# Token-major value projections: all 512 columns at once in four PSUM banks, instead of 256 columns per two heads

## The chip, the cores and the metric

The kernel runs on one core of a Trainium2 chip. The metric is the device time of one execution in microseconds. The median of three runs before the change is 1900.26 us (1900.05 to 1903.23).

## The reference, cut to what matters

Two layers of a hybrid block run over 256 latent tokens (`x`) and 256 context tokens (`y`), and a second block of feed-forward, recurrent and gating mixers follows them. Each layer projects the normalised tokens to queries, keys, values and gates of three attentions. The change touches the values of two of them, the retention (4 heads of 128 columns) and the neighbourhood attention (8 heads of 64 columns):

```python
rq, rk, rv, rg, nq, nk, nv, ng, gq, gk, gv, gg, mg = split_cols(hx @ w_in)
crq, crk, crv, crg, cnq, cnk, cnv, cng, cgq, cgk, cgv, cgg, cmg = split_cols(hy @ w_in)
o_lat, o_ctx = bidir_retention(heads(rq, 4), heads(rk, 4) * ksc, heads(rv, 4),
                               heads(crq, 4), heads(crk, 4) * ksc, heads(crv, 4), log_g, need_ctx)
na_x = neighbourhood_attention(heads(nq, 8), heads(nk, 8), heads(nv, 8), heads(cnk, 8), heads(cnv, 8), na_rpb, rows)
```

`rv` with `crv`, and `nv` with `cnv`, are each a product of 512 tokens by 1024 features with 1024 by 512 weights, once per layer.

## The kernel before

Matrices are kept to nearly fp32 precision as a high and a low part: a product is three matmuls (high by high, high by low, low by high), which `mm3` issues. Weights are loaded as `raw` tiles of 2048 columns (three buffers); `wsplit` makes the high part (`wh`) on ScalarE by a cast and the low part (`wl`) on VectorE by a subtraction, in pieces of 128 by 1024 (four buffers each). PSUM has eight tiles of 512 columns (`ps`), one bank each. Everything else lives in 60 tiles of 128 by 512 (`r`).

Most projections (`project`) put the weights in the array and stream tokens, so features come out on the partitions. Values are needed token-major, so `values` does it the other way round: a block of 128 tokens (`xh`, `xl`) stands in the array and the weights are streamed. It was called for two heads of the retention at once (tasks r0 and r2, 256 columns) and for two pairs of heads of the neighbourhood attention (tasks n0 and n2, 256 columns): four calls per layer, eight in all. In a call each of four token blocks takes 8 feature tiles, hence 4 x 8 x 3 = 96 matmuls of 256 columns; two token blocks share a bank. Each 256-column result is then split into high and low parts (`pair` for the retention, a strided `split` for the neighbourhood attention).

Tasks are generators: `t_ret` (r0 to r3), `t_na` (n0 to n3), `t_gkv` (gk) and `t_gqa` (g0 to g3, the grouped attention), `t_merge` (m0 to m2, gates and output projections of the three branches), `t_ada`. Layer 0 wants the order r, n, g, layer 1 the order r0 g0 r1 g1 and so on, then n. In layer 1 only the 256 latent tokens have queries. The recorder keeps every instruction with its dependencies, and a list scheduler with its own cost table then writes the order of each engine's queue; on the chip each queue is followed in that order. In layer 0 the first six projections of r0 and r1 (`lead`) accumulate in six banks ahead of everything else. Every instruction has the line of a helper, L335, so the trace is read by the tile names: `L0r` is layer 0's retention, `L1n` layer 1's neighbourhood attention, `L0m` its merges, `f`, `fa`, `fb`, `mix` the second block.

Of the kernel before, what the change touches and what calls it, by code (L numbers as in the profile page):

```python
# [13 lines left out]
P = 128  # L14
# [3 lines left out]
NK = D // P  # L18
# [21 lines left out]
def _turns(order, first, rate):  # L40
# [11 lines left out]
OFF = {  # L52
    "rq": 0, "rk": 512, "rv": 1024, "rg": 1536, "nq": 2048, "nk": 2560, "nv": 3072, "ng": 3584,
    "gq": 4096, "gk": 4608, "gv": 4736, "gg": 4864, "mg": 5376,
}
# [282 lines left out]
class _K:  # L338
# [22 lines left out]
    def ps(self):  # L361
        return self.tile("ps", 512)
# [213 lines left out]
    def values(self, l, c0, hx, stacked, out):  # L576


        (raw,) = self.wload([self.wk(self.a["w_in"][l], c0, 256)])
        ws = self.wsplit(raw[:, :4, :]) + self.wsplit(raw[:, 4:, :])  # L580
        for t2 in range(2):
            ps = self.ps()
            for t in range(2):
                tk = slice((2 * t2 + t) * P, (2 * t2 + t + 1) * P)
                for k in range(NK):
                    xh, xl = hx[k]
                    self.mm3(ps[:, 256 * t : 256 * t + 256], (xh[:, tk], xl[:, tk]), ws[k], k == 0, k == NK - 1)
            for t in range(2):
                src = ps[:, 256 * t : 256 * t + 256]
                if not stacked:  # L590
                    out.append(self.pair(src, 256))
                else:
                    v = self.r()
                    hl = v.rearrange("p (a x c) -> p a x c", a=2, x=4)
                    self.split(hl[:, :, 0::3, :], hl[:, :, 1:3, :], src.rearrange("p (a e c) -> p a e c", a=2, e=2))
                    out.append(v)
            yield 0

    def in_tiles(self, l, names):

# [65 lines left out]
    def ret_av(self, h, v, px, pc, nq):  # L666

        nc = self.nc
        col = P * (h % 2)
        vt = [(v[t][0][:, col : col + P], v[t][1][:, col : col + P]) for t in range(4)]  # L670
        o = self.ps()
        for kt in range(2):
            self.mm3(o[:, :nq], vt[2 + kt], (pc[kt][0][:, :nq], pc[kt][1][:, :nq]), kt == 0, False)
        for kt in range(2):
            c = slice(256 * kt, 256 * kt + 256)
            self.mm3(o[:, :T], vt[kt], (px[0][:, c], px[1][:, c]), False, kt == 1)
        oc, mu = self.f(), self.f()
        nc.scalar.copy(oc[:, :nq], o[:, :nq])
        nc.gpsimd.partition_all_reduce(mu[:, :nq], oc[:, :nq], channels=P, reduce_op=RED.add)
        self.stt(oc[:, :nq], mu[:, :nq], -1.0 / P, oc[:, :nq], ALU.mult, ALU.add)  # L680
        sq = self.f()
        self.act(sq[:, :nq], oc[:, :nq], AF.Square)
        nc.gpsimd.partition_all_reduce(mu[:, :nq], sq[:, :nq], channels=P, reduce_op=RED.add)
        return oc, mu
# [234 lines left out]
    def t_ret(self, l, h, hx, nq, S):  # L919
        yield from self.turn(S, "r", h)  # L920
        names = [(n, h) for n in ("rk", "rq", "rg")]
        led = self.led if l == 0 else {}
        raw = dict(zip([n for n in names if n not in led], self.in_tiles(l, [n for n in names if n not in led])))
        ps = lambda n, c: led[n, h] if (n, h) in led else self.project(raw[n, h], hx, c)

        def values():
            if h % 2 == 0:
                S["rv"] = v = []
                yield from self.values(l, OFF["rv"] + P * h, hx, False, v)

        if l == 0:
            yield from values()
            k = self.pair(ps("rk", T2), T2, KSC)
            yield 0
        q = self.pair(ps("rq", nq), nq)
        yield 0
        g = self.silu2(ps("rg", nq), nq)
        yield 0
        if l == 1:
            yield from values()  # L940
            k = self.pair(ps("rk", T2), T2, KSC)
            yield 0
        v = S["rv"]
        px, pc = self.ret_scores(l, h, q, k, nq)
        yield 6
        cen, vs = self.ret_av(h, v, px, pc, nq)
        S["done"] += 1
        yield 8
        S["o0"].append(self.ret_out(l, h, cen, vs, g, nq))

    def t_na(self, l, p, hx, nq, S):
        a = self.a
        yield from self.turn(S, "n", p)
        if p % 2 == 0:
            S["nv"] = v = []
            yield from self.values(l, OFF["nv"] + P * p, hx, True, v)
        v = S["nv"]
        wk, wq, wg = self.in_tiles(l, [("nk", p), ("nq", p), ("ng", p)])
        kp = self.project(wk, hx, T2)
        ks = [self.stack(kp, T2, r) for r in (0, 64)]  # L960
        yield 0
        qp = self.project(wq, hx, nq)
        qk = []
        los = self.zero_halves((0, 64), nq)
        for e, r in enumerate((0, 64)):
            qd = self.double(qp, nq, r, los[e][r : r + 64], 0.125)
            qk.append([(ks[e], qd), (ks[e], los[e])])
        yield 0
        g = self.silu2(self.project(wg, hx, nq), nq)
        yield 0  # L970
        pr = []
        for e in range(2):
            bias = self.tile("b", 384)
            self.nc.sync.dma_start(bias, a["na"][l, 2 * p + e])
            pr.append(self.scores(qk[e], nq, bias, 1.0, True))
            yield 3 if e == 0 else 14
        c0 = 256 * (p % 2)
        yield from self.attend(S, pr, v, (c0, c0 + P), g, nq, "o1", True)
# [659 lines left out]
```

## Time and profile before

| | before |
|---|---|
| median of three runs | 1900.26 us |
| the profiled execution | 1902.64 us, span 1900.9 us |
| TensorE matmul busy | 1858.4 us, 98% |
| VectorE busy | 1432.9 us, 75% |
| ScalarE busy | 1066.3 us, 56% |
| GpSimd busy | 209.7 us, 11% |
| mean granted TensorE clock | 0.994 of full speed |

The span runs from the first instruction to the last. Matmuls are pipelined and their ends are modelled, so a stream of matmuls is priced here by the distance from one start to the next and not by the mean duration of one. The two layers of the first block lie between about 64 us and 973 us; from there to the end the second block runs.

### The profile page before, as it was taken

How to read it: one execution, taken by the hardware profiler on the slowest of the kernel's cores; microseconds unless marked ns; L12 is line 12 of the kernel's file. 1: busy time of each engine (PE TensorE's matmuls, PEld its weight loads, DVE VectorE, ACT ScalarE, POOL GpSimd, SP SyncE). 2: the span in 40 equal slices, each digit the busy share in tenths (PEclk: the TensorE clock that was granted, in tenths of full speed). 3: DMA queues.
4: the chain of work that ended last, by engine and by line, in shares of the span. 5: the costliest groups of instructions: out<-in, count | busy, mean ns of one | idle time of the engine just before them, and what ended most of it. 6: DMA issues, size and time to landing. Idle time of an engine off the chain costs nothing.

```text
span 1900.9 us, 33415 instructions
## 1 busy us (share of the span) xinstructions
PE 1858.4 (98%) x13632; PEld 1739.5 (92%) x13632; DVE 1432.9 (75%) x2177; ACT 1066.3 (56%) x1704; POOL 209.7 (11%) x152
## 2 busy tenths in 40 slices
PE   6999999999999999999999999999999999999998
PEld 4888777777789889999999999999999999999998
DVE  7778978799857699999787668876656665777654
ACT  4656555656445597766565447754445444755443
POOL 0123323133300022222000000000000010000000
PEclk9999999999999999999999999999999999999999
DMA  9332443524343324434655566355555555545552
GB/s 321 119 97 93 128 148 101 155 88 123 102 153 100 89 78 116 124 106 146 209 178 188 190 194 200 111 201 187 179 183 180 188 181 193 190 157 176 181 188 98
DMA packets 336249, 291.95 MB, mean 154 GB/s; under 512 B 9184, under 2 KB 325728, under 8 KB 336096
## 3 DMA queue, kind: packets, MB, share of 16 engines
q1 hardware_dynamic: 336096, 289.82, 48.0%
q8 instruction: 107, 1.75, 0.4%
q14 instruction: 46, 0.38, 0.1%
HBM read 288.75 MB, written 1.05 MB: 152 GB/s over the span
## 4 chain that ended last, share of the span: by engine, by line
PE 87%; DVE 8%; ACT 2%; issue 1%; POOL 1%; DMA 0%; SPq 0%; DVEq 0%; POOLq 0%; ACTq 0%
PE fb_ps L335 13%; PE L0m_ps L335 7%; PE f_ps L335 7%; PE fa_ps L335 7%; PE L0n_ps L335 5%; PE L1m_ps L335 5%; PE L1r_ps L335 4%; PE L0r_ps L335 4%; PE fb1b_ps L335 3%; PE L1n_ps L335 3%; PE fa1b_ps L335 3%; PE fb0b_ps L335 3%; PE f0b_ps L335 3%; PE mix_ps L335 3%; PE L0out_ps L335 2%; PE L0in_ps L335 2%
## 5 line engine op out<-in xcount | busy, mean ns | idle before, releaser
L335 PE MATMUL fb_ps<-fb_r,fb_wh 128*128 128x256 f32 x1408 | 253.8, 283 | 0.0
L335 PEld LDWEIGHTS fb_ps<-fb_r,fb_wh 128*128 128x128 f32 x1408 | 219.6, 192 | 0.1
L335 PE MATMUL fb_ps<-fb_r,fb_wl 128*128 128x256 f32 x704 | 198.9, 283 | 0.0
L335 ACT CAST fb_wh<-fb_raw 128x1024 fp32r<-128x1024 f32 x88 | 92.2, 1047 | 123.0 <-PE fb_ps L335 89.3
L335 DVE TENSOR_TENSOR fb_wl<-fb_raw,fb_wh 128x1024 fp32r<-128x1024 f32 x88 | 107.7, 1224 | 65.1 <-ACT fb_wh L335 65.0
L335 PEld LDWEIGHTS fb_ps<-fb_r,fb_wl 128*128 128x128 f32 x704 | 135.0, 192 | 0.0
L335 PE MATMUL f_ps<-f_r,f_wh 128*128 128x256 f32 x704 | 127.2, 283 | 0.0
L335 PE MATMUL fa_ps<-fa_r,fa_wh 128*128 128x256 f32 x704 | 126.9, 283 | 0.0
L335 PE MATMUL L0m_ps<-L0in_r,L0m_wh 128*128 128x512 f32 x384 | 121.5, 395 | 0.0
L335 PEld LDWEIGHTS f_ps<-f_r,f_wh 128*128 128x128 f32 x704 | 109.8, 192 | 0.1
L335 PEld LDWEIGHTS fa_ps<-fa_r,fa_wh 128*128 128x128 f32 x704 | 109.8, 192 | 0.1
L335 PE MATMUL fa_ps<-fa_r,fa_wl 128*128 128x256 f32 x352 | 99.4, 283 | 0.0
L335 PE MATMUL f_ps<-f_r,f_wl 128*128 128x256 f32 x352 | 99.3, 283 | 0.0
L335 PEld LDWEIGHTS L0m_ps<-L0in_r,L0m_wh 128*128 128x128 f32 x384 | 71.9, 189 | 16.7 <-issue 1.6
L335 ACT CAST fa_wh<-fa_raw 128x1024 fp32r<-128x1024 f32 x44 | 46.1, 1047 | 63.5 <-PE fa_ps L335 39.7
L335 DVE TENSOR_TENSOR fa_wl<-fa_raw,fa_wh 128x1024 fp32r<-128x1024 f32 x44 | 53.8, 1224 | 35.4 <-ACT fa_wh L335 35.4
L335 POOL MEMSET mix_r<- 128x128 f32 (+1 forms) x36 | 7.7, 239 | 653.4 <-DVE fa_r L335 490.4
L335 DVE TENSOR_TENSOR L0g_r<-L0g_r,L0g_r 128x512 f32<-128x512 f32 (+3 forms) x116 | 72.4, 670 | 7.6 <-ACT L0g_r L335 5.4
L335 ACT CAST f_wh<-f_raw 128x1024 fp32r<-128x1024 f32 x44 | 46.1, 1048 | 56.4 <-PE f_ps L335 35.6
L335 PE MATMUL L0m_ps<-L0in_r,L0m_wl 128*128 128x512 f32 x192 | 75.0, 391 | 0.0
L335 ACT ACT_TABLE_LOAD x56 | 71.8, 1283 | 3.1 <-PE L0out_ps L335 1.4
L335 DVE TENSOR_TENSOR f_wl<-f_raw,f_wh 128x1024 fp32r<-128x1024 f32 x44 | 53.7, 1221 | 24.9 <-ACT f_wh L335 24.8
(506 smaller groups left out, 5729.7 us busy)
## 6 DMA issues: line engine op xcount, KB each, us to landing
fb_raw<-in_ffn_w_in_dram SPq DMA_DIRECT2D x44, 1024.0 KB, 5.2
f_raw<-in_ffn_w_in_dram SPq DMA_DIRECT2D x22, 1024.0 KB, 5.1
fa_raw<-in_ffn_w_in_dram SPq DMA_DIRECT2D x22, 1024.0 KB, 5.2
ada_raw<-in_ada_w_dram SPq DMA_DIRECT2D x32, 512.0 KB, 4.5
L0m_raw<-in_w_in_dram SPq DMA_DIRECT2D x24, 512.0 KB, 3.9
L1m_raw<-in_w_in_dram SPq DMA_DIRECT2D x24, 512.0 KB, 4.3
L0in_raw<-in_ada_w_dram SPq DMA_DIRECT2D x32, 256.0 KB, 6.0
f0b_raw<-in_ffn_w_out_dram SPq DMA_DIRECT2D x8, 1024.0 KB, 5.3
```

The costliest lines, as they stand in the source:

```text
L335: getattr(getattr(self.real, eng), method)(*a, **k)
```

## The change

`values` is called once per layer and attention, for all 512 columns (tasks r0 and n0), four calls in all instead of eight. It takes four banks at once, one for each token block. The weights come in two loads of four feature tiles by 512 columns; within one load, two feature tiles at a time go to all four banks, so the feature tiles are in the outer loop: 4 x 8 x 3 = 96 matmuls of 512 columns per call. The retention's results are split 512 columns at a time into two tiles, the neighbourhood attention's as before in 256-column pieces. r1 to r3 and n1 to n3 take their columns from what r0 and n0 left.

```diff
--- before.py
+++ after.py
@@ -576,25 +576,32 @@
     def values(self, l, c0, hx, stacked, out):
 
 
-        (raw,) = self.wload([self.wk(self.a["w_in"][l], c0, 256)])
-        ws = self.wsplit(raw[:, :4, :]) + self.wsplit(raw[:, 4:, :])
-        for t2 in range(2):
-            ps = self.ps()
-            for t in range(2):
-                tk = slice((2 * t2 + t) * P, (2 * t2 + t + 1) * P)
-                for k in range(NK):
-                    xh, xl = hx[k]
-                    self.mm3(ps[:, 256 * t : 256 * t + 256], (xh[:, tk], xl[:, tk]), ws[k], k == 0, k == NK - 1)
-            for t in range(2):
-                src = ps[:, 256 * t : 256 * t + 256]
-                if not stacked:
-                    out.append(self.pair(src, 256))
-                else:
+        w = self.a["w_in"][l]
+        pss = [self.ps() for _ in range(4)]
+        for k0 in range(0, NK, 4):
+            (raw,) = self.wload([self.wk(w, c0, 512, k0, 4)])
+            ws = self.wsplit(raw[:, :2, :]) + self.wsplit(raw[:, 2:, :])
+            for k2 in (0, 2):
+                for t, ps in enumerate(pss):
+                    tk = slice(t * P, (t + 1) * P)
+                    for k in (k0 + k2, k0 + k2 + 1):
+                        xh, xl = hx[k]
+                        self.mm3(ps, (xh[:, tk], xl[:, tk]), ws[k - k0], k == 0, k == NK - 1)
+            if k0 == 0:
+                yield 0
+        for ps in pss:
+            if not stacked:
+                out.append(self.pair(ps, 512))
+            else:
+                vs = []
+                for i in range(2):
                     v = self.r()
                     hl = v.rearrange("p (a x c) -> p a x c", a=2, x=4)
-                    self.split(hl[:, :, 0::3, :], hl[:, :, 1:3, :], src.rearrange("p (a e c) -> p a e c", a=2, e=2))
-                    out.append(v)
-            yield 0
+                    src = ps[:, 256 * i : 256 * i + 256].rearrange("p (a e c) -> p a e c", a=2, e=2)
+                    self.split(hl[:, :, 0::3, :], hl[:, :, 1:3, :], src)
+                    vs.append(v)
+                out.append(vs)
+        yield 0
 
     def in_tiles(self, l, names):
 
@@ -666,7 +673,7 @@
     def ret_av(self, h, v, px, pc, nq):
 
         nc = self.nc
-        col = P * (h % 2)
+        col = P * h
         vt = [(v[t][0][:, col : col + P], v[t][1][:, col : col + P]) for t in range(4)]
         o = self.ps()
         for kt in range(2):
@@ -924,9 +931,9 @@
         ps = lambda n, c: led[n, h] if (n, h) in led else self.project(raw[n, h], hx, c)
 
         def values():
-            if h % 2 == 0:
+            if h == 0:
                 S["rv"] = v = []
-                yield from self.values(l, OFF["rv"] + P * h, hx, False, v)
+                yield from self.values(l, OFF["rv"], hx, False, v)
 
         if l == 0:
             yield from values()
@@ -951,10 +958,10 @@
     def t_na(self, l, p, hx, nq, S):
         a = self.a
         yield from self.turn(S, "n", p)
-        if p % 2 == 0:
+        if p == 0:
             S["nv"] = v = []
-            yield from self.values(l, OFF["nv"] + P * p, hx, True, v)
-        v = S["nv"]
+            yield from self.values(l, OFF["nv"], hx, True, v)
+        v = [vs[p // 2] for vs in S["nv"]]
         wk, wq, wg = self.in_tiles(l, [("nk", p), ("nq", p), ("ng", p)])
         kp = self.project(wk, hx, T2)
         ks = [self.stack(kp, T2, r) for r in (0, 64)]
```

Three places show how the order of the queues moves. The first is TensorE's queue where layer 0's retention begins, right behind the last of the lead's matmuls (`L0in`); `L0r0_ps` are the banks of the values. Before:

```order
L335 MATMUL L0in_ps_35_127<-L0in_r_85_177,L0in_r_101_193 128x512
L335 MATMUL L0r0_ps_107_199<-L0r0_wh_103_195,L0in_r_25_117 128x256
L335 MATMUL L0r0_ps_107_199<-L0r0_wl_104_196,L0in_r_25_117 128x256
L335 MATMUL L0r0_ps_107_199<-L0r0_wh_103_195,L0in_r_26_118 128x256
L335 MATMUL L0r0_ps_107_199<-L0r0_wh_103_195,L0in_r_28_120 128x256
L335 MATMUL L0r0_ps_107_199<-L0r0_wl_104_196,L0in_r_28_120 128x256
L335 MATMUL L0r0_ps_107_199<-L0r0_wh_103_195,L0in_r_29_121 128x256
L335 MATMUL L0r0_ps_107_199<-L0r0_wh_103_195,L0in_r_44_136 128x256
L335 MATMUL L0r0_ps_107_199<-L0r0_wl_104_196,L0in_r_44_136 128x256
```

After:

```order
L335 MATMUL L0in_ps_35_127<-L0in_r_85_177,L0in_r_101_193 128x512
L335 MATMUL L0r0_ps_102_194<-L0r0_wh_107_199,L0in_r_25_117 128x512
L335 MATMUL L0r0_ps_102_194<-L0r0_wl_108_200,L0in_r_25_117 128x512
L335 MATMUL L0r0_ps_102_194<-L0r0_wh_107_199,L0in_r_26_118 128x512
L335 MATMUL L0r0_ps_102_194<-L0r0_wh_107_199,L0in_r_28_120 128x512
L335 MATMUL L0r0_ps_102_194<-L0r0_wl_108_200,L0in_r_28_120 128x512
L335 MATMUL L0r0_ps_102_194<-L0r0_wh_107_199,L0in_r_29_121 128x512
L335 MATMUL L0r0_ps_103_195<-L0r0_wh_107_199,L0in_r_25_117 128x512
L335 MATMUL L0r0_ps_103_195<-L0r0_wl_108_200,L0in_r_25_117 128x512
```

A bank got 48 matmuls of 256 columns in a row (two token blocks); now each of four banks gets six of 512 columns in turn, four rounds.

The second place is VectorE's queue in layer 0 where pair n1's probabilities are finished and n2 begins. `L0n2_wl` are the low parts of n2's weights, from `raw_404` the values' and from `raw_415` the keys' and queries'. Before:

```order
L335 TENSOR_TENSOR L0n1_r_370_462<-L0n1_r_362_454,L0n1_r_369_461 128x512
L335 TENSOR_TENSOR L0n1_r_366_458<-L0n1_r_363_455,L0n1_r_365_457 128x512
L335 TENSOR_TENSOR L0n0_r_374_466<-L0n0_ps_373_465,L0n0_r_374_466 64x512
L335 TENSOR_TENSOR L0n2_wl_406_498<-L0n2_raw_404_496,L0n2_wh_405_497 128x1024
L335 TENSOR_TENSOR L0n1_r_372_464<-L0n1_r_372_464,L0n1_r_363_455 128x256
L335 TENSOR_TENSOR L0n0_r_374_466<-L0n0_r_374_466,L0n0_r_300_392 128x512
L335 TENSOR_TENSOR L0n1_r_372_464<-L0n1_r_372_464,L0n1_r_363_455 128x256
L335 TENSOR_TENSOR L0n2_wl_408_500<-L0n2_raw_404_496,L0n2_wh_407_499 128x1024
L335 TENSOR_TENSOR L0n0_r_376_468<-L0n0_r_374_466,L0n0_r_375_467 128x512
L335 TENSOR_TENSOR L0n2_wl_419_511<-L0n2_raw_415_507,L0n2_wh_418_510 128x1024
```

After:

```order
L335 TENSOR_TENSOR L0n1_r_381_473<-L0n1_r_373_465,L0n1_r_380_472 128x512
L335 TENSOR_TENSOR L0n1_r_377_469<-L0n1_r_374_466,L0n1_r_376_468 128x512
L335 SCALAR_TENSOR_TENSOR L0n0_r_311_403<-L0n0_r_311_403,L0n0_r_295_387 128x512
L335 TENSOR_TENSOR L0n0_r_385_477<-L0n0_ps_366_458,L0n0_r_385_477 64x512
L335 TENSOR_TENSOR L0n0_r_385_477<-L0n0_ps_384_476,L0n0_r_385_477 64x512
L335 TENSOR_TENSOR L0n1_r_383_475<-L0n1_r_383_475,L0n1_r_374_466 128x256
L335 TENSOR_TENSOR L0n2_wl_419_511<-L0n2_raw_415_507,L0n2_wh_418_510 128x1024
L335 TENSOR_TENSOR L0n0_r_385_477<-L0n0_r_385_477,L0n0_r_311_403 128x512
L335 TENSOR_TENSOR L0n1_r_383_475<-L0n1_r_383_475,L0n1_r_374_466 128x256
L335 TENSOR_TENSOR L0n2_wl_424_516<-L0n2_raw_415_507,L0n2_wh_423_515 128x1024
```

The two splits of n2's value weights are gone from here (they stand ahead of n0 now), and the split of its key weights comes in their place.

The third place is TensorE's queue in layer 1 between the last scores of g0 (`L1g0_ps`) and the first scores of g1 (`L1g1_ps_1277`); `L1r2` is the third head's projections. Before:

```order
L335 MATMUL L1g0_ps_1269_1361<-L1g0_r_1248_1340,L1gk_r_1210_1302 128x256
L335 MATMUL L1g0_ps_1269_1361<-L1g0_r_1246_1338,L1gk_r_1210_1302 128x256
L335 MATMUL L1g0_ps_1269_1361<-L1g0_r_1248_1340,L1gk_r_1210_1302 128x256
L335 MATMUL L1g0_ps_1269_1361<-L1g0_r_1246_1338,L1gk_r_1210_1302 128x256
L335 MATMUL L1g1_ps_1277_1369<-L1g1_r_1265_1357,L1gk_r_1210_1302 128x256
L335 MATMUL L1g1_ps_1279_1371<-L1g1_r_1265_1357,L1gk_r_1210_1302 128x256
L335 MATMUL L1g1_ps_1287_1379<-L1g1_r_1266_1358,L1gk_r_1210_1302 128x256
L335 MATMUL L1g1_ps_1277_1369<-L1g1_r_1264_1356,L1gk_r_1210_1302 128x256
```

After:

```order
L335 MATMUL L1g0_ps_1280_1372<-L1g0_r_1257_1349,L1gk_r_1221_1313 128x256
L335 MATMUL L1g0_ps_1280_1372<-L1g0_r_1259_1351,L1gk_r_1221_1313 128x256
L335 MATMUL L1g0_ps_1280_1372<-L1g0_r_1257_1349,L1gk_r_1221_1313 128x256
L335 MATMUL L1r2_ps_1320_1412<-L0out_r_1064_1156,L1r2_wh_1321_1413 128x512
L335 MATMUL L1r2_ps_1320_1412<-L0out_r_1065_1157,L1r2_wh_1321_1413 128x512
L335 MATMUL L1r2_ps_1316_1408<-L0out_r_1064_1156,L1r2_wh_1317_1409 128x256
L335 MATMUL L1r2_ps_1316_1408<-L0out_r_1065_1157,L1r2_wh_1317_1409 128x256
L335 MATMUL L1r2_ps_1316_1408<-L0out_r_1064_1156,L1r2_wl_1318_1410 128x256
L335 MATMUL L1r2_ps_1316_1408<-L0out_r_1067_1159,L1r2_wh_1317_1409 128x256
L335 MATMUL L1r2_ps_1316_1408<-L0out_r_1068_1160,L1r2_wh_1317_1409 128x256
```

Before, the scores of g1 follow those of g0 directly. Now fifteen matmuls of r2's projections stand between them, two of 512 columns and thirteen of 256, and behind g1's scores r2's values, 96 matmuls of 256 columns, are gone.

## Rows read from the trace of the kernel before

**Rows 1.** The page: busy time of each engine, and the granted clock in 40 slices.

```profile
PE 1858.4 (98%) x13632; PEld 1739.5 (92%) x13632; DVE 1432.9 (75%) x2177; ACT 1066.3 (56%) x1704; POOL 209.7 (11%) x152
...
PEclk9999999999999999999999999999999999999999
```

**Rows 2.** The page: chain that ended last, shares of the span by engine.

```profile
PE 87%; DVE 8%; ACT 2%; issue 1%; POOL 1%; DMA 0%; SPq 0%; DVEq 0%; POOLq 0%; ACTq 0%
```

**Rows 3.** Windows of the first block: stretch, length, busy us, granted clock, DMA.

```profile
core 0: us, PE busy (x) PEld busy (x) DVE busy (x) ACT busy (x) POOL busy (x), PEclk, DMA share, GB/s
64.50:184.00 119.50, 119.50 (x701) 105.12 (x700) 89.68 (x119) 62.94 (x95) 34.38 (x15) 1.00 0.30 91
184.00:222.00 38.00, 35.16 (x205) 26.57 (x204) 37.84 (x51) 23.66 (x40) 18.23 (x8) 1.00 0.37 110
222.00:395.00 173.00, 171.53 (x892) 136.84 (x891) 141.82 (x195) 97.02 (x152) 43.45 (x23) 1.00 0.42 127
...
683.00:697.00 14.00, 10.78 (x61) 10.27 (x61) 12.68 (x32) 12.21 (x24) 2.43 (x2) 0.76 0.27 75
697.00:816.00 119.00, 118.30 (x876) 112.51 (x876) 112.09 (x181) 89.17 (x159) 25.84 (x23) 1.00 0.40 115
```

**Rows 4.** Groups by shape, TensorE: the value matmuls of layer 0's retention.

```profile
L335 PE MATMUL L0r_ps<-L0r_wh,L0in_r 128*128 128x256 f32 x128 | 23.7, 283 | 0.0
...
L335 PE MATMUL L0r_ps<-L0r_wl,L0in_r 128*128 128x256 f32 x64 | 18.1, 283 | 0.0
```

**Rows 5.** The chain in order of time: start us, us, what; unbroken streams of one shape.

```profile
474.89 16.32 PE L0m_ps L335 x72
...
894.17 56.16 PE L1m_ps L335 x468
```

**Rows 6.** The chain again, from 60 to 260 us: the lead's end and n2's start.

```profile
59.80 4.76 PE L0in_ps L335 x21
...
64.56 15.72 PE L0r_ps L335 x120
...
220.38 27.37 PE L0n_ps L335 x158
```

**Rows 7.** Timeline of VectorE and ScalarE: start us, us, instruction, idle before.

```profile
63.72 0.68 DVE L335 TENSOR_TENSOR L0r_r<-L0in_ps,L0r_r 128x512 fp32r<-128x512 f32 x1
...
152.37 0.42 DVE L335 TENSOR_TENSOR L0n_r<-L0n_ps,L0n_r 128x256 fp32r<-128x256 f32 x1
...
164.22 1.21 DVE L335 TENSOR_TENSOR L0n_wl<-L0n_raw,L0n_wh 128x1024 fp32r<-128x1024 f32 x1
...
150.84 0.37 ACT L335 CAST L0n_r<-L0n_ps 128x256 fp32r<-128x256 f32 x1
...
156.67 1.28 ACT L335 ACT_TABLE_LOAD   x1
```

**Rows 8.** Timeline of TensorE: its longer waits, in brackets the idle time and releaser.

```profile
206.44 0.62 PE L335 MATMUL L0n_ps<-L0n_r,L0n_r 128*128 128x256 f32 x3 [1.01 <-DVE L0n_r L335]
...
217.98 0.39 PE L335 MATMUL L0n_ps<-L0n_wl,L0in_r 128*128 128x256 f32 x1 [0.37 <-DVE L0n_wl L335]
...
421.21 0.67 PE L335 MATMUL L0g_ps<-L0g_r,cstt 128*128 128x256 f32 x2 [3.55 <-DVE L0g_r L335]
...
508.05 0.80 PE L335 MATMUL L0m_ps<-L0g_r,L0m_wh 128*128 128x512 f32 x1 [3.82 <-ACT L0g_r L335]
...
687.95 0.50 PE L335 MATMUL L1g_ps<-L1g_r,L1gk_r 128*128 128x256 f32 x2 [1.86 <-ACT L1g_r L335]
```

**Rows 9.** Window of n2 of layer 0, columns as in group 3.

```profile
222.00:250.00 28.00, 28.00 (x169) 23.91 (x168) 22.60 (x32) 11.81 (x20) 2.47 (x3) 1.00 0.42 131
```

## The prediction

> **What bounds the kernel now.** I read the page first: TensorE is busy 98% of the span, VectorE 75%, ScalarE 56%, and the granted clock is full in every slice [rows 1]. Busy time of pipelined matmuls overstates, so the second view is the chain of work that ended last: 87% of it is TensorE, 8% VectorE [rows 2]. The reader is to see that a microsecond of matmul work taken out is mostly a microsecond off the span, except where TensorE waits. The third view, windows of the first block, says where that is [rows 3]: from 64.5 to 184 us TensorE has no gap; from 184 to 222 it lacks 2.84 us while VectorE is busy 37.84 of 38.00; from 683 to 697 it lacks 3.22 us and the granted clock falls to 0.76. The timeline names the larger single waits, and I come to them with the moves.
>
> **What is removed.** Layer 0's retention issues 128 + 64 = 192 value matmuls of 256 columns [rows 4]; there are four such groups (two layers, two attentions), so 768 matmuls of 256 columns become 384 of 512. Prices come from unbroken streams on the chain [rows 5]: 72 matmuls of 512 columns took 16.32 us, 0.2267 us each; 468 of 256 took 56.16 us, 0.1200 us each. Two of 256 cost 0.2400, so each pair saves 0.0133 us. Hence 768 x 0.1200 = 92.16 us, 384 x 0.2267 = 87.05 us, saving 5.1 us, 1.28 us per group. The new loop goes to another bank every six matmuls; the lead already does that with 512 columns, and its last 21 took 4.76 us, again 0.2267 each [rows 6], so I add nothing for it. The bounds of this term are 0 (if a value matmul of 512 columns took twice 0.1200) and 5.1; I take 5.1, because both prices are of these very shapes.
>
> The page "TensorE: Matmul & The Clock Gate" of the Trainium skill, section "Back-to-back issue gap", puts the isolated distance at columns / 2.4 GHz plus about 2.5 ns. By it a pair would save only 2.5 ns and the change 1.0 us, an estimate from that page. The streams here do not agree: they stand 13.3 ns above columns / 2.4 GHz at both widths, so the measured rows decide.
>
> **What costs nothing.** *Banks:* the lead holds six of eight. Values start at 64.56 [rows 6], the third bank is wanted 12 x 0.2267 = 2.7 us later. Four of the lead's banks have been read out by 63.72 + 0.68 = 64.4 us [rows 7], so four are there. Without that cover the price is the delay of the readout, up to about 2 us. *Readout:* the retention's results take four VectorE subtractions of 512 columns (0.68) for eight of 256 (0.42) per layer [rows 7], 2.7 us for 3.4; nobody waits for values at once, the scores come first. *ScalarE:* the queue holds 54 table loads for 56, at 1.28 us [rows 7]; ScalarE is idle 44% of the time. *Loads:* the same bytes, in two loads of the same size, the second pulled ahead to r0 or n0; the transfers' share is 0.27 to 0.42 in the windows of the first block [rows 3]. *Second block:* from the first feed-forward on, the queues are in the same order on every engine.
>
> **What moves.** Each group takes 96 x 0.1200 = 11.5 us of TensorE work, with 2 x 1.21 + 4 x 0.42 = 4.1 us of VectorE work [rows 7], from r2 or n2 to r0 or n0. Everything between the two starts 96 x 0.2267 - 96 x 0.1200 - 1.28 = 9.0 us later in the second attention of a layer and 10.2 in the first; behind r2 or n2 TensorE is level again, less the saving. Two places matter, because VectorE is nearly full there.
>
> *n2 of layer 0.* TensorE waits 1.01 us for n1's probabilities and 0.37 for n2's value weights [rows 8]. n1 is the same work for both engines, only later, so those waits stay. Behind it stood the value matmuls, the first 96 of the 158 in the stream of 27.37 us [rows 6], in which VectorE could catch up. VectorE has 28.00 - 22.60 = 5.4 us free from 222 to 250 [rows 9], and 4.1 us of work leaves. TensorE could stand 11.5 - 5.4 - 4.1 = 2.0 us; the bounds are 0 and 11.5 - 4.1 = 7.4 (VectorE without any free time). The queue puts n2's key weights straight where the value weights were, which speaks for the low end: I take +1.
>
> *r2 of layer 1.* From 697 to 816 VectorE is busy 112.09 of 119.00 [rows 3], so 6.9 us are free, over a longer stretch; bounds again 0 and 7.4. Key and gate projections of r3, g2 and n0 can be pulled forward, I take +1. Just ahead of it, g1's scores wait 1.86 us at 687.95 [rows 8]; now fifteen of r2's projections (13 x 0.1200 + 2 x 0.2267 = 2.0 us) stand in that gap. The whole hole is 14.0 us for 61 matmuls [rows 3], at most 14.0 - 61 x 0.1200 = 6.7 us with the fallen clock; bounds 0 and 6.7. I take -2, the fill itself.
>
> The two long waits of layer 0 (3.55 us at 421, 3.82 at 508 [rows 8]) belong to the grouped attention, whose distances in the queue stay as they were: 0.
>
> **Sum.** -5.1 + 1 + 1 - 2 = -5.1 us. The profiled execution took 1902.64 us (span 1900.9), 2.4 above the median; it should become 1897.5, the median 1900.26 - 5.1 = 1895.2 us.
>
> **Rivals.** 0.2% of the time, 3.8 us, is about what a measurement of this kernel can tell from no change: faster is below 1896.5, slower above 1904.1.
>
> 1. *The saving arrives, the waits cancel* (the forecast): 1892 to 1896.4. For it: 98% and 87% TensorE.
> 2. *A wait takes part of it back:* the 2.0 us at n2, 2.0 at r2 and nothing gained at g1, 1900.26 - 5.1 + 4.0 = 1899.2. For it: VectorE 37.84 of 38.00; against it: the work ahead of those waits shrinks by 4.1 us too.
> 3. *The hole in layer 1 closes:* up to 6.7 us more, 1900.26 - 5.1 - 6.7 = 1888.5. For it: the fill; against it: the ScalarE chain that g1 waits for is no shorter.
> 4. *The change does not do what it says:* a value matmul of 512 columns costs as much as two of 256, saving 0, 1900.3. Against it: the same shapes in the streams. By the page cited above the time would be 1899.3, an estimate; the streams speak against it too.
> 5. *Slower:* at r2 of layer 1 VectorE is the limit and there is no filler. From 683 to 697 waits of 3.22 us made a hole of up to 6.7, since the granted clock fell: a wait there costs about twice its length. The forecast turns to slower once r2's waits pass (5.1 + 3.8) / 2 = 4.5 us; at 5 us the time is 1900.26 - 5.1 + 10 = 1905.2. For it: VectorE's 112.09 of 119.00; against it: the projections that can be pulled forward.
>
> **Chances.** Forecast 0.45, the second 0.30, the third 0.13, the fourth 0.03, slower 0.09 (its point is far, but VectorE is near it). Faster is 0.45 + 0.13 = 0.58, the same 0.30 + 0.03 = 0.33, slower 0.09. The range 1890 to 1901.5 leaves out the slower case, about a third of the third case and the upper end of the second, under 0.2 in all.
>
> **What would show it.** 13632 - 384 = 13248 matmuls, value groups of 96 with 512 columns and a distance of 0.2267 us between starts; a longer distance makes the first term wrong. In layer 0 no new wait at about 67 us; at the start of n2's projections a wait of at most 2 us. In layer 1 g1's scores wait less than 1.86 us, and no clock below full between r2 and n0; a fallen clock there is the slower case. The stretch from the end of the first block on stays as long as it was; if it changes, the prediction is wrong for a reason that I have not seen.

## The result, and the profile after

The changed kernel took 1913.72 us (median of four runs, 1912.11 to 1914.71) against 1901.72 us: a ratio of 1.0062, interval 1.0045 to 1.008. It is slower by 12 us where 5 us faster were forecast. The profiled execution took 1914.71 us, its span is 1912.9 us.

The page after, in the lines that answer to [rows 1, 2]:

```profile
PE 1860.5 (97%) x13248; PEld 1724.8 (90%) x13248; DVE 1436.6 (75%) x2169; ACT 1063.4 (56%) x1694; POOL 195.9 (10%) x152
...
PE   6999999999999999989999999999999999999998
...
PE 86%; DVE 7%; ACT 3%; issue 1%; DMA 1%; POOL 0%; SPq 0%; DVEq 0%; ACTq 0%; POOLq 0%
```

The 384 matmuls are gone, yet busy shares and chain look as before. One digit of the page hints at the loss: in the 18th of its 40 slices, from 813 to 861 us, TensorE is busy 8 tenths (before: 9). Where the 12 us went is told by two marks in the timeline: the last output projection of layer 0 (`L0m`) and that of layer 1 (`L1m`) on TensorE. From the first value matmul to the first mark, and from there to the second, each in the profiled execution:

| | layer 0, us | layer 1, us |
|---|---|---|
| before | 502.7 | 382.9 |
| after | 501.7 | 395.5 |

Layer 0 gained 1.0 us, layer 1 lost 12.5. Behind it nothing changed.

The waits of TensorE after, its longest groups: engine and tile, what it waited for, us in total, times, longest.

```profile
PE L1n_ps L335 <- DVE L1n_r L335: 6.5, 1, 6.5
PE L1g_ps L335 <- ACT L1g_r L335: 3.9, 2, 2.6
PE ada_ps L335 <- DMA ada_raw<-in_ada_w_dram: 3.8, 1, 3.8
PE L0n_ps L335 <- ACT L0n_r L335: 3.6, 1, 3.6
```

The timeline of TensorE after, values first, then the long waits:

```profile
64.87 0.39 PE L335 MATMUL L0r_ps<-L0r_wh,L0in_r 128*128 128x512 f32 x1
...
69.86 0.39 PE L335 MATMUL L0r_ps<-L0r_wl,L0in_r 128*128 128x512 f32 x1
...
697.31 0.51 PE L335 MATMUL L1g_ps<-L1g_r,L1gk_r 128*128 128x256 f32 x2
...
700.91 0.75 PE L335 MATMUL L1g_ps<-L1g_r,L1gk_r 128*128 128x256 f32 x4 [0.58 <-DVE L1gk_r L335]
...
704.46 0.55 PE L335 MATMUL L1g_ps<-L1g_r,L1gk_r 128*128 128x256 f32 x1 [2.57 <-ACT L1g_r L335]
...
757.19 0.50 PE L335 MATMUL L1g_ps<-L1g_r,L1gk_r 128*128 128x256 f32 x2 [1.36 <-ACT L1g_r L335]
...
849.36 0.77 PE L335 MATMUL L1n_ps<-L0out_r,L1n_wh 128*128 128x256 f32 x2 [6.45 <-DVE L1n_r L335]
```

Between the first two rows lie 22 matmuls with three changes of bank: 4.99 / 22 = 0.2268 us each, as in the streams of before [rows 5]. So the width does what it should, and there is no wait at its start. The last row is the new thing: in layer 1, a projection of pair n2 waits 6.45 us for VectorE.

The rows between are told apart by count, since each pair of the grouped attention has 16 score matmuls and g0's end at 694.5 us. The 16 of g1 begin at 697.31, and only the last four of them wait, 0.58 us: the projections put in front of them did fill the wait of 1.86 us [rows 8]. The matmul at 704.46 is the first product of g0's probabilities with the values. It waits 2.57 us for ScalarE, which still works on g0's softmax; before, r2's projections and r2's values were TensorE's work during that time.

Windows of layer 1 after (columns as in [rows 3]):

```profile
697.00:710.00 13.00, 9.79 (x47) 8.05 (x46) 12.58 (x27) 11.92 (x23) 2.86 (x4) 0.74 0.14 40
750.00:770.00 20.00, 16.79 (x108) 15.60 (x106) 18.00 (x33) 17.49 (x33) 6.36 (x6) 0.83 0.19 57
...
780.00:800.00 20.00, 20.00 (x90) 16.58 (x89) 17.15 (x29) 10.94 (x21) 1.06 (x1) 1.00 0.37 106
800.00:810.00 10.00, 10.00 (x75) 9.52 (x74) 4.27 (x6) 4.67 (x8) 0.31 (x1) 1.00 0.08 19
810.00:849.00 39.00, 32.78 (x229) 30.45 (x227) 38.60 (x64) 27.37 (x50) 8.74 (x7) 0.97 0.44 126
...
845.00:850.00 5.00, 0.64 (x3) 0.67 (x4) 4.91 (x9) 3.61 (x8) 0.00 (x0) 0.66 0.26 82
850.00:855.00 5.00, 5.00 (x31) 5.00 (x31) 4.01 (x10) 1.20 (x3) 1.79 (x1) 0.66 0.07 23
```

The first five stretches before:

```profile
697.00:710.00 13.00, 13.00 (x105) 12.69 (x105) 11.63 (x20) 12.83 (x25) 4.01 (x4) 1.00 0.43 122
750.00:770.00 20.00, 19.47 (x153) 18.50 (x152) 19.78 (x36) 19.46 (x35) 5.50 (x6) 1.00 0.46 133
...
780.00:800.00 20.00, 20.00 (x143) 18.78 (x142) 19.39 (x33) 14.14 (x26) 1.68 (x1) 1.00 0.39 118
800.00:810.00 10.00, 10.00 (x67) 9.16 (x66) 9.91 (x17) 6.65 (x11) 2.40 (x4) 1.00 0.51 149
810.00:849.00 39.00, 38.03 (x293) 36.65 (x292) 38.37 (x67) 23.75 (x47) 9.68 (x6) 1.00 0.32 94
```

Read these in pairs. From 697 to 710 TensorE was busy throughout before; now it lacks 3.21 us and the granted clock falls to 0.74. From 800 to 810, behind n0's values, while n0's other projections run, VectorE now idles (busy 4.27 of 10 us, in the same time before 9.91); then it is full for 39 us, and TensorE, which was busy 38.03 us in that time before, is busy 32.78.

The chain that led to the wait after, start, us, what:

```profile
810.88 0.70 DVE L1n_r L335
...
838.17 2.04 DVE L1n_r L335 x3
840.21 1.14 DVE L1m_wl L335
...
842.02 1.26 DVE L1n_r L335 x3
...
847.48 1.01 DVE L1n_r L335 x2
...
848.52 0.70 DVE L1n_r L335
...
849.36 6.82 PE L1n_ps L335 x40
```

From 810.88 to the end of the wait it runs on VectorE almost alone. What TensorE waits for is a bank: in the compiled program n2's gate projection takes the bank that held n2's keys. The instruction at 848.52 is the last that reads them, a split that stands behind n1's softmax in VectorE's queue. The 40 matmuls behind the wait took 6.82 us instead of 40 x 0.12 = 4.80, since the granted clock had fallen (0.66 from 845 to 855): the hole costs 6.45 + 2.0 = 8.5 us.

### The profile page after: what moved, and what is told of

Its sections match the earlier page's. It is cut to its first block, busy times and chain, and to the rows that moved or that the text cites. A ratio compares the mean times of both kernels' runs of the same rounds, so it can differ in the third digit from the quotient of the medians.

```text
span 1912.9 us, 32631 instructions
## 1 busy us (share of the span) xinstructions
PE 1860.5 (97%) x13248; PEld 1724.8 (90%) x13248; DVE 1436.6 (75%) x2169; ACT 1063.4 (56%) x1694; POOL 195.9 (10%) x152
## 4 chain that ended last, share of the span: by engine, by line
PE 86%; DVE 7%; ACT 3%; issue 1%; DMA 1%; POOL 0%; SPq 0%; DVEq 0%; ACTq 0%; POOLq 0%
PE fb_ps L335 13%; PE L0m_ps L335 8%; PE f_ps L335 7%; PE fa_ps L335 7%; PE L0n_ps L335 6%; PE L1m_ps L335 5%; PE L0r_ps L335 4%; PE L1r_ps L335 3%; PE fb1b_ps L335 3%; PE fa1b_ps L335 3%; PE fb0b_ps L335 3%; PE f0b_ps L335 3%; PE L1n_ps L335 3%; PE mix_ps L335 3%; PE L0out_ps L335 2%; PE L0in_ps L335 2%
## 5 line engine op out<-in xcount | busy, mean ns | idle before, releaser
L335 DVE TENSOR_TENSOR L0g_r<-L0g_r,L0g_r 128x256 f32<-128x256 f32 (+3 forms) x116 | 74.9, 687 | 8.2 <-ACT L0g_r L335 5.6
L335 PE MATMUL L1m_ps<-L0out_r,L1m_wh 128*128 128x256 f32 x384 | 72.8, 286 | 0.0
```

Source lines behind the costliest of these rows:

```text
L335: getattr(getattr(self.real, eng), method)(*a, **k)
```

## The experiments

Three theories stood at the start. *Cover*: the value matmuls at r2 and n2 were what TensorE did while VectorE and ScalarE worked on the scores; without them it waits. *The loop*: four banks, bank changes and wide readouts cost wherever they stand. *The plan*: the scheduler's order shifts as a whole, and no part has a price. Ratios are to the kernel before, run beside each.

**e1, e2, e3: one part of the change each.** `values2` is the old function; e1 has the sets below, e2 `{"r": (1,), "n": ()}`, e3 `{"r": (), "n": (1,)}`.

```diff
+WIDE = {"r": (0,), "n": (0,)}
...
-            if h == 0:
+            if h == 0 and l in WIDE["r"]:
                 S["rv"] = v = []
                 yield from self.values(l, OFF["rv"], hx, False, v)
+            elif h % 2 == 0 and l not in WIDE["r"]:
+                S["rv"] = v = []
+                yield from self.values2(l, OFF["rv"] + P * h, hx, False, v)
```

> Layer 0 has the new values (512 columns at r0 and n0), layer 1 the old ones (256 columns at r0, r2, n0, n2). Theory (the loss is made in layer 1, where work that filled TensorE beside a busy VectorE was taken away from r2 and n2): layer 0 ended 0.5 us earlier after the change, so this kernel takes about 1901.2 us against 1901.7, no difference. Rival (the new loop itself costs, by four banks held at once, a bank change every six matmuls, or the results read 512 columns at a time): two of the four groups carry half of the 12 us, 1907.7 us.

Measured: 1899.96 us, ratio 0.9987 (0.9977 to 0.9996).

> Only the retention of layer 1 has the new values. In the trace after the change TensorE lost 10.9 us against the price of its matmuls from 640 us to the first value matmuls of n0, before 3.6 us. Theory: this group alone carries 7.3 - 1.3 = 6.0 us, 1907.7 us, and the holes lie between g0 and g3. Rival (the new loop itself): a quarter of 12 us, 1904.7 us. Second rival (the whole plan shifts, no part has a cost of its own): any other number, and the parts do not add up to 12.

Measured: 1907.35 us, ratio 1.0026 (1.0016 to 1.0036). Its timeline has the holes of the changed kernel at the same places:

```profile
705.84 0.55 PE L336 MATMUL L1g_ps<-L1g_r,L1gk_r 128*128 128x256 f32 x1 [2.57 <-ACT L1g_r L336]
...
758.57 0.50 PE L336 MATMUL L1g_ps<-L1g_r,L1gk_r 128*128 128x256 f32 x2 [1.36 <-ACT L1g_r L336]
```

> Only the neighbourhood attention of layer 1 has the new values. In the trace after the change TensorE lost 9.4 us against the price of its matmuls from n0's values to 912 us, before 1.7 us in the same stretch of the program. Theory: this group alone carries 7.7 - 1.3 = 6.4 us, 1908.1 us, with a wait of 5 to 7 us for VectorE behind n1. Rival (the new loop itself): a quarter of 12 us, 1904.7 us. Second rival (the whole plan shifts): the three parts do not add up to 12.

Measured: 1909.06 us, ratio 1.0036 (1.0023 to 1.0049), with a wait of 6.44 us behind n1. In the profiled executions layer 1 is 6.7 us longer in e2 and 5.5 in e3, together 12.2 of the 12.5; layer 0 is 3.3 us shorter in e1. Such lengths, from one execution each, are uncertain by 2 to 3 us: e1 and the changed kernel have the same order of matmuls in layer 0 and differ by 2.3 us there, and e2's profiled execution took 3.2 us more than its median. By the ratios the parts are -2.5, +4.9 and +6.9 us, together 9.3, where the whole is 11.8; the difference lies within the intervals. So the parts add up as far as can be told, and nothing is left that only the plan as a whole would explain. Equal shares per group are out: the change in layer 0 alone is a gain.

**e4: the move without the width.**

```diff
+                if h == 0:
+                    S["rvs"] = [[], []]
+                    for i in range(2):
+                        yield from self.values(l, OFF["rv"] + 256 * i, hx, False, S["rvs"][i])
+                S["rv"] = S["rvs"][h // 2]
```

(the same for n, with p)

> The old loop with 256 columns, two banks and token blocks outside, but both calls stand at r0 and at n0, as in the changed kernel: the move alone, 768 matmuls of 256 columns. Theory (the move costs 17 us, the width gives 5.1 back): 1913.7 + 5.1 = 1918.8 us, between 1917 and 1921. Rival (the new loop itself costs): about 1901.7 us, as before.

Measured: 1919.84 us, ratio 1.0087 (1.0072 to 1.0102). The old loop at the new places costs the most, so the place is the cause and the loop is not. The width gives back the difference to the changed kernel: in ratios 0.0025 x 1902 = 4.8 us, where 5.1 were computed (the two intervals together allow 0.4 to 9).

**e7: two banks at a time.**

```diff
-        pss = [self.ps() for _ in range(4)]
+        ws, pss = [], []
         for k0 in range(0, NK, 4):
             (raw,) = self.wload([self.wk(w, c0, 512, k0, 4)])
-            ws = self.wsplit(raw[:, :2, :]) + self.wsplit(raw[:, 2:, :])
+            ws += self.wsplit(raw[:, :2, :]) + self.wsplit(raw[:, 2:, :])
+        for t2 in range(2):
+            two = [self.ps() for _ in range(2)]
...
```

> The changed kernel, but its values take two banks at a time: all eight feature tiles of 512 columns are split first, then the token blocks 0 and 1 are multiplied, then 2 and 3; 384 matmuls of 512 columns as in the changed kernel, at the same places. Theory (the move to r0 and n0 costs): no difference from 1913.7 us beyond 2 us. Rival (four banks held at once take the banks from the projections): 5 us or more below it, 1908 us or less.

Measured: 1913.12 us (1909.88 to 1914.91), ratio 1.0051 (1.0036 to 1.0066). No difference, and the same wait in its list:

```profile
PE L1n_ps L335 <- DVE L1n_r L335: 6.5, 1, 6.5
```

**e9, e10: other work for TensorE in the old places.** `fill` multiplies token tiles by each other into two banks that nobody reads.

```diff
+    def fill(self, hx):
+        for t2 in range(2):
+            ps = self.ps()
...
+                    self.mm3(ps[:, 256 * t : 256 * t + 256], (xh[:, tk], xl[:, tk]), (xh[:, :T], xl[:, :T]), k == 0, k == NK - 1)
...
+        if l == 1 and p == 2:
+            self.fill(hx)
+            yield 0
```

> The kernel of e3 (new values in the neighbourhood attention of layer 1 alone, 1909.1 us) with 96 extra matmuls of 256 columns ahead of n2's projections, where the old values stood: token blocks by token blocks, into two banks that nobody reads, no weights, no VectorE or ScalarE work; 96 x 0.12 = 11.5 us of added TensorE work. Theory (TensorE has no work to cover the softmax of n1, a chain through VectorE, GpSimd and ScalarE): the added work lies in the hole of 6.4 us and the 1.9 us of fallen clock behind it, so it costs only 11.5 - 8.3 = 3.2 us: 1912.3 us, and the wait behind n1 is under 1 us. Rival (the chain is tied to what TensorE does, and moves with it): 1909.1 + 11.5 = 1920.6 us.

Measured: 1912.01 us, ratio 1.0044 (1.0029 to 1.0059) against e3's 1.0036: 11.5 us of added matmuls cost about 1.5 us by the ratios (4.3 by the length of layer 1). Nothing waits at n2 any more (a merge ahead of it waits 1.07 us), and the chain runs through n2 on TensorE alone:

```profile
830.37 26.58 PE L1n_ps L336 x200
856.95 2.88 PE L1m_ps L336 x24
```

This is the plainest evidence for cover: work that touches no other engine fits into the hole.

> The kernel of e2 (new values in the retention of layer 1 alone, 1907.4 us) with the same 96 extra matmuls behind r2's gate projection, where the old values stood; 11.5 us of added TensorE work. In e2 TensorE lost about 7.3 us more than before between g0 and g3. Theory (cover, as at n2): most of the loss goes, 1907.4 + 11.5 - 6 = 1913 us, between 1911.5 and 1915. Rival (in the retention the loss has another cause than missing cover, as the order of the queues between g1 and r2): 1907.4 + 11.5 = 1919 us.

Measured: 1914.99 us, ratio 1.0062 (1.0047 to 1.0077) against e2's 1.0026: 0.0036 x 1903 = 6.9 us for 11.5, so 4.6 us of the loss is cover, at the upper edge of what was expected. The wait of g0's product, 2.57 us in e2, is gone. Part of the loss stays: g1's scores, ahead of the fill, wait again, and so does a merge behind r2:

```profile
697.72 1.22 PE L336 MATMUL L1g_ps<-L1g_r,L1gk_r 128*128 128x256 f32 x8 [1.37 <-DVE L1g_r L336]
...
772.23 0.50 PE L336 MATMUL L1m_ps<-L1r_r,L1m_wh 128*128 128x256 f32 x2 [2.19 <-ACT L1r_r L336]
```

**e5: useful work as cover.** To e3 is added:

```diff
+for _p, _m in enumerate((0, 4, 8, 12)):
+    TURN[1]["n"][_p] = (TURN[1]["n"][_p][0], _m)
```

> The kernel of e3 (new values in the neighbourhood attention of layer 1 alone; +6.5 us), with one more edit: in layer 1 the pairs n0 to n3 begin after 0, 4, 8 and 12 steps of the merges, not after -4, 0, 4 and 8. Four merge steps, 4 x 48 x 0.12 = 23.0 us of matmuls with about 2.4 us of VectorE work each, come ahead of n1 instead of behind n3. Theory (the wait of 6.4 us behind n1 is VectorE's lag, because the moved value matmuls no longer give TensorE work while VectorE catches up): any other filler serves too; VectorE gains 23.0 - 9.6 = 13.4 us on TensorE, the wait and the fallen clock behind it (6.4 + 1.9 us) go, and the time comes to about 1901, between 1899 and 1903. Rival (the wait is made by the four banks held at once, or by the readout in 512 columns): the new loop is the same, 1909 us.

Measured: 1901.34 us, ratio 0.9991 (0.9982 to 1.0001). 0.0045 x 1902 = 8.6 us better than e3, with the same loop at the same place.

**e6, e13: what the wait hangs on.** The order of every queue is that of the changed kernel; instructions are cut as they are issued, so most scores keep their maximum (e13 cuts the exponential too, and most scores go without it).

```diff
                 self.tt(v2(e), v2(e), mb, ALU.subtract)
+                nc.ops[-1].cut = self.st.startswith("L1n")
...
+            if self.ops[i].cut:
+                a = [x[:, :, :16] for x in a]
```

> The changed kernel with the same order on every engine; only, the 16 subtractions of the maximum (128 by 512) in the neighbourhood attention of layer 1 are cut on VectorE to 16 of 256 columns in each half, so most scores keep their maximum. Eight of them stand in the stretch from 811 to 849 us, 6.1 us together; cut they should take about 0.1 us each, so VectorE is 5.3 us earlier at the end of it. Theory (VectorE's lag makes the wait of 6.45 us): the wait falls to about 1.2 us, the fallen clock behind it gives back up to 1.9 us more, 1913.7 - 5.3 - 1.9 = 1906.5 us, between 1905 and 1909. Rival (the wait is for something that VectorE only happens to release, as banks held by the values or a load): no less than 1912 us.

Measured: 1913.11 us, ratio 1.005 (1.0033 to 1.0067). My expectation fell: the wait is 5.0 us, 1.4 shorter and not 5.3, and of that the clock took 0.8 back. Its chain, with the rows that answer to 810.88 and 849.36 above:

```profile
829.44 0.42 DVE L1n_r L337
...
848.21 7.66 PE L1n_ps L337 x40
```

40 matmuls in 7.66 us lose 2.9 where the changed kernel lost 2.0. VectorE's unbroken run begins at 829.44 now, behind TensorE and ScalarE, and not at 810.88: what it gained in n0 is gone when it has to wait for n1's scores. That only n1's four subtractions then count is how I read it, not measured by itself.

> As e6, the changed kernel in the same order with the subtractions of the maximum cut in layer 1's neighbourhood attention, and now the 16 exponentials behind them too, on ScalarE from 512 to 32 columns; most scores get neither. In e6 the stretch ahead of the wait went through ScalarE from 838.9 to 846.6 us. Theory (TensorE waits for a chain that goes through VectorE and ScalarE in turns, so that what counts is the chain of the one pair n1, not the sum of VectorE's work): four exponentials of 0.62 us stand in it, cut to about 0.2, so the wait falls from e6's 5.0 to about 3.3 us and the time to about 1910.5 us, between 1909 and 1912. Rival (neither engine's work sets it): as e6, 1913 us.

Measured: 1908.91 us (1905.12 to 1911.22, more scatter than elsewhere), ratio 1.0033 (1.0022 to 1.0043), just under the expected 1909 to 1912. The wait falls further, to 4.0 us, with VectorE's work no smaller than in e6:

```profile
842.79 1.37 DVE L1m_wl L337 x2
...
845.51 0.70 DVE L1n_r L337
...
846.35 6.53 PE L1n_ps L337 x40
```

So ScalarE's part of n1's chain counts as well: 6.45, 5.0, 4.0 us. The wait is not VectorE's backlog alone, nor n1's softmax alone. In e13 TensorE is through with n2's queries at 842.35, and the split that frees the bank begins at 845.51; of the time between, the low parts of two merge weights take 1.37 us on VectorE (842.79).

**e12: another order on VectorE.**

```diff
+            cap = self.nc.cap
+            if l == 1:
+                self.nc.cap = 0
             qd = self.double(qp, nq, r, los[e][r : r + 64], 0.125)
+            self.nc.cap = cap
```

> The kernel of e3 with one edit of the planner: in layer 1's neighbourhood attention the splits of the query projections, which release the bank that the gate projection waits for, get a due time 25 us earlier, so VectorE does them ahead of the softmax of the pair before. Theory (missing cover): TensorE then waits in other places for the same chain, and the time stays within 3 us of 1909.1 us. Rival (it is only the order in VectorE's queue, the split that frees the bank stands behind the softmax): the hole of 6.4 + 1.9 us goes, 1901 to 1903 us.

Measured: 1906.77 us, ratio 1.0018 (1.0009 to 1.0028) against e3's 1.0036: 3.4 us of some 8 come back. Both were partly right. The split that frees the bank did stand too far back; with the query splits in front, the new plan gives the gate projection the bank of n2's queries, where the changed kernel and e3 gave it that of the keys. TensorE still waits for it, only less, and a little in another place:

```profile
841.58 0.77 PE L336 MATMUL L1n_ps<-L0out_r,L1n_wh 128*128 128x256 f32 x2 [2.35 <-DVE L1n_r L336]
...
853.81 0.50 PE L336 MATMUL L1m_ps<-L1r_r,L1m_wh 128*128 128x256 f32 x2 [0.67 <-ACT L1n_r L336]
```

**e8, e11, e14: a version that keeps the cover.** e8 takes the new values without layer 1's retention, with e5's edit and, for layer 0:

```diff
-TURN = [_turns("r0 r1 r2 r3 n0 n1 n2 n3 g0 g1 g2 g3", 5, 2),
+TURN = [_turns("r0 r1 r2 r3 n0 n1 n2 n3 g0 g1 g2 g3", 4, 2),
```

e11 is that schedule with the old values everywhere, e14 with the new ones everywhere.

> New values in layer 0 and in the neighbourhood attention of layer 1, the retention of layer 1 as before; the pairs of layer 1's neighbourhood attention begin after 0, 4, 8 and 12 merge steps as in e5, and in layer 0 every task begins two merge steps later than it did. Theory: the width of three groups, 3 x 1.28 = 3.8 us, arrives, the filler in layer 1 is back, layer 0 keeps the waits of e1 (which took 2.6 us off with its two groups): about 1899 us against 1902.6, faster than both kernels. Rival (the loss at n belongs to the new loop): 1902.6 - 2.6 + 6.5 = 1906.5 us.

Measured: 1894.25 us (1893.68 to 1894.73) against 1902.8, ratio 0.9954 (0.9939 to 0.9969): faster than both kernels, and 4.8 us below what was expected.

> The kernel before, its values untouched, with e8's two edits of the schedule: layer 0's tasks begin two merge steps later, and layer 1's pairs n0 to n3 after 0, 4, 8 and 12 steps. It tells what of e8's 8.5 us is the schedule's own. Theory (e8's gain is 3.8 us of width and the rest is layer 0's schedule): 1902.7 - 4.7 = 1898 us. Rival (the schedule gives nothing without the new values): 1902.7 us.

Measured: 1901.48 us, ratio 0.9987 (0.9978 to 0.9997): between the two expected times and nearer to the rival.

> All four groups with the new values, as in the changed kernel, under e8's two edits of the schedule. It differs from e8 in layer 1's retention alone. Theory (the retention of layer 1 keeps its lack of cover, since the schedule offers it no merge steps there): 1894.3 + 4.8 = 1899 us, between 1897 and 1901. Rival (the schedule as a whole was what the changed kernel lacked): 1893 us, e8 less 1.3 us of width.

Measured: 1899.7 us, ratio 0.9982 (0.9973 to 0.9992): layer 1's retention costs 0.0028 x 1902 = 5.3 us against e8, as it did in e2 (4.9). Its longest wait in layer 1 is that of e2:

```profile
PE L1g_ps L337 <- ACT L1g_r L337: 3.9, 2, 2.6
```

Of e8's 8.5 us, 2.5 are the schedule's own (e11) and 3.8 the width of three groups; 2.2 are left by this sum. By layers, in the profiled executions, e8 is 6.0 us shorter in layer 0 (e11 3.0, e1 3.3: there schedule and new values simply add) and 2.5 in layer 1 (e5 2.0, while e11 is 1.7 longer: there the merge steps help only with the new values).

## Why the prediction was wrong, point by point

- **Width, -5.1.** Right: 0.2268 us a matmul in the values, 4.8 us between e4 and the changed kernel. The distance that the page "TensorE: Matmul & The Clock Gate" of the Trainium skill (section "Back-to-back issue gap") gives for an isolated matmul would have made it 1.0 us, an estimate. The distances measured here speak against it; the 4.8 us alone, at 0.4 to 9, would not.
- **Banks, bank changes, readout: 0.** Right: no wait at 65 us, and e7 changes nothing.
- **n2 of layer 0, +1.** The sum came out, by luck. Layer 0 gained 1.0 us in the changed kernel and 3.3 in e1, of 2.6 saved. But n2's projections do not wait at all. The wait for n1's probabilities, which was to stay at 1.01 us, is 3.58, and a load at 380 us costs 3.83, against "loads cost nothing". The two long waits of the grouped attention, which were to stay, fell from 3.55 to 0.83 and from 3.82 to 0.77 and made up for it. One reading was off without changing the sum: n2's values had begun before the stream of 158 matmuls at 220.38 us (the row at 217.98 [rows 8] is one of them), so only 78 of them are in it, not 96.
- **"Two places matter, because VectorE is nearly full there."** This step failed first. There are three places: n2 of layer 1 has the same loss of 11.5 us of matmuls, and I gave it nothing; the stretch I read ended at 816 us. By e3 it cost 0.0036 x 1902 = 6.9 us net, 5.5 by the length of layer 1; with the 1.3 saved, 6.8 to 8.2 us of waits and fallen clock.
- **r2 of layer 1, +1, and the fill at g1, -2.** The sum of the two failed too: instead of -1, waits and fallen clock cost 4.9 + 1.3 = 6.2 us by e2's ratio, 6.7 + 1.3 = 8.0 by the length of its layer 1. At g1's scores the fill did what it should (0.58 us for 1.86). What the prediction left out is that the projections put there, and the values taken away, had been the cover of g0's softmax just behind: g0's product now waits 2.57 us. So the hole moved: 9.79 busy us of 13.00 at a clock of 0.74, against 10.78 of 14.00 at 0.76 before [rows 3], and a second one opened at 757 us (0.83 from 750 to 770). The larger waits there are for ScalarE (2.57 and 1.36 us), where the prediction looked at VectorE's free time.
- **The method behind both.** I set what TensorE loses against the time that VectorE is free in a long stretch (5.4 us, 6.9 us). The waits are shorter-sighted. One pair's scores go through VectorE, GpSimd and ScalarE; what counts is how long that one chain takes, with whatever stands in the queue ahead of the instruction that TensorE waits for (e6, e12, e13), and whether TensorE has other work for just that time (e5, e9, e10). VectorE's free time elsewhere, as at 800 us, is lost.
- **Slower, 0.09.** The fifth rival named r2 of layer 1 and the clock's share, and its sign came: a fallen clock between r2 and n0 (0.74 and 0.83). But its price was 5 us instead of 12, since n2 was not in it.

What stays open: how n1's chain splits between VectorE, GpSimd and ScalarE (GpSimd's part was not tried), what each of the instructions ahead of the split in VectorE's queue is worth, and what keeps about 2 us of e2's loss when r2 is filled.

## What to carry to other kernels

Merging two small pieces of matmul work into one large piece saves its 13 ns a pair, and takes away the work that the second piece did under another stage's softmax; price each place that loses work, all of them, before the saving. Ask at each how long the chain of that one step takes on the other engines and what TensorE has left for that time, not how busy an engine is on average. If the plan has movable work (here the merge steps), move it into the gap along with the change: the same four groups then went from +12 us to -3.4 (e14), and three of them to -8.5 (e8); 2.5 us of either is what the moved work gives without the change (e11). If the wait is for a bank, look also at what stands ahead of the instruction that frees it (e12).

## What the runs showed of the hardware

A wait costs more than its length, and not in proportion. After 6.45 us the next 40 matmuls lost 2.0 us, after 5.0 us 2.9, after 4.0 us 1.7. What decides is not the wait but how long the clock stays at the low level behind it. From the end of the wait in the changed kernel, in e6 and in e13 (length, busy us of PE, PEld, DVE, ACT and POOL, granted clock, DMA):

```profile
849.36:853.40 4.04, 4.04 (x19) 4.04 (x20) 3.88 (x9) 0.41 (x1) 1.79 (x1) 0.50 0.25 88
```

```profile
848.21:854.20 5.99, 5.99 (x28) 5.99 (x29) 4.51 (x11) 1.09 (x3) 1.79 (x1) 0.50 0.16 56
```

```profile
846.35:849.80 3.45, 3.45 (x16) 3.45 (x17) 3.29 (x7) 0.41 (x1) 1.23 (x1) 0.51 0.33 115
```

Behind these stretches the granted clock is 0.99 to 1.00. Half of each, 2.0, 3.0 and 1.7 us, is what the 40 matmuls lost. So a wait that ends earlier can cost more behind it, as in e6.

At the low level the distance is 0.64 us for three matmuls of 256 columns, 0.2133 each, in the timeline after:

```profile
850.14 0.63 PE L335 MATMUL L1n_ps<-L0out_r,L1n_wh 128*128 128x256 f32 x2
850.57 0.41 PE L335 MATMUL L1n_ps<-L0out_r,L1n_wl 128*128 128x256 f32 x1
850.78 0.63 PE L335 MATMUL L1n_ps<-L0out_r,L1n_wh 128*128 128x256 f32 x2
```

That is 256 / 1.2 GHz with nothing above it, while at the high level 13.3 ns stand above 256 / 2.4 GHz. That the fixed part is hidden at the low level is also what the page "TensorE: Matmul & The Clock Gate" of the Trainium skill states (section "Wait — 56ns, not 53.3ns?"). The trace agrees in this; for the high level the page has about 2.5 ns, where the rows here show 13.3.
